# One PSUM tile for a pair of heads' scores, filling passes tied two attention steps up, and a gate phase without GpSimd, in a three-mixer decoder layer on one core

## Chip, core, metric

One core of a Trainium2 chip runs the whole kernel. The metric is the time of one execution on the device, in microseconds (us). The engines are called by name or by the profile's short names: TensorE (PE, with its weight loads as PEld), VectorE (DVE), ScalarE (ACT), GpSimd (POOL), SyncE (SP, which issues the transfers).

## What is computed

One pre-norm layer over 512 tokens of width 1024, float32 throughout. Three attention mixers run side by side on the normalised input, each with eight heads of 64: A (block-sparse; with 512 tokens it is plain causal attention), B (three dilated sliding windows, mixed by their softmax denominators) and C (window 128, two shared key heads, learned sinks). Each mixer's output is multiplied by a SiLU gate, projected to 1024, multiplied by a sigmoid gate, summed with the others and projected once more:

```python
branches = jnp.stack([o_a.reshape(b, s, W_BR) * jax.nn.silu(ga),
                      o_b.reshape(b, s, W_BR) * jax.nn.silu(gb),
                      o_c.reshape(b, s, W_BR) * jax.nn.silu(gc)], axis=2)
br = jnp.einsum('bsiw,iwd->bsid', branches, w_branch[l])
gates = jax.nn.sigmoid(gate_logits.reshape(b, s, N_BRANCH, D_MODEL))
merged = jnp.sum(gates * br, axis=2)
x = x + jnp.einsum('bsd,de->bse', merged, w_out[l])
```

## The kernel before

**Arithmetic.** Every float32 operand of a matmul is split in two fp32r parts: `hi` (a rounding copy, `split_hi`, on ScalarE, line 131) and `lo = x - hi` (`split_lo`, line 136, on VectorE or GpSimd). A product is three passes: hi with hi, hi with lo, lo with hi. All weights go through this split once, in `load_w`, which gives every fourth `lo` (every second for three jobs) to GpSimd.

**Stages.** The start normalises x and transposes it (`start_x`) and makes the bias table (`start_bias`). Then ten attention units run in the order A0 W0 R0 Z0 A1 W1 R1 Z1 C0 C1; each is one half (four heads) of mixer A, of one of B's three windows (W, R, Z), or of C. A unit is projected (`unit_project`, lines 484 to 486 are its passes) and then attended: A and W by `pair_attention`, R and Z by `residue_attention`, C by `shared_attention`. Last comes the gate phase: a list of jobs, each a product of x with 512 columns of gate weights (`gl`, `raw`) or a branch product with `w_branch` (`br`), and the output projection (line 1069).

**An attention step.** In `pair_attention`, `scores(p, t)` takes one 128-row block t of two heads e = 0, 1, which lie on rows 0 to 63 and 64 to 127: three passes for each, written in turns (line 639), into two PSUM tiles of one bank under the tag `sc`, of which there are two buffers. VectorE adds the bias and takes the row minimum (line 568), ScalarE exponentiates (line 569), TensorE transposes the result (line 659), both engines split it, and `weigh_values` multiplies by the values (line 594). A half unit has 8 `scores` steps: p = 0, 1 and t = 0 to 3. Their width is 256 columns in W, and 256, 256, 384, 512 in A. `residue_attention` writes one bank per head for all four t (line 735); `shared_attention` takes a new `sc` tile for every block (lines 701 and 702).

**Order of the work.** Instructions are traced in program order and queued by the builder's scheduler: on each engine, what is ready by its own clock goes first, earlier-traced ones before later ones. The next unit's projection is a generator of three passes at a time ("filling"). For the units in `RATION` some of it is traced ahead, and the rest between the steps, a share after each; `issue_after` allows those passes only behind the step's last TensorE instruction:

```python
for pe in steps:
    got += share
    with tc.issue_after(pe.ins):
        while got >= 1:
            next(fill, None)
            got -= 1
```

C0 and C1 are filled with the first gate columns (`raw_columns`).

**The gate phase.** From the third job on, the products of 512 x 1024 by 1024 x 512 are made from seven smaller ones (Strassen-like, `fast_cols`, line 347): `fast_x` makes combinations of x once, `fast_weights` makes combinations of each job's weights and splits them (lines 291 to 299 and 136). Of a job's seven `lo` parts three are GpSimd's, as is one subtraction (line 296); of `fast_x`, three sums (line 311) and two `lo` parts. `fast_cols` sums the products out of PSUM banks a, b, c, d (lines 364 to 381; c has the tag `sc`). `silu` multiplies sigmoid by the raw gate on GpSimd (line 993) and by the mixer's output on VectorE (line 994). The branch products go to four banks, one of them `sc` (lines 1041 to 1043), and are gated at lines 1049 to 1052.

GpSimd keeps, before and after, the power for the norms (line 142), the sums of B's outputs (line 968) and memsets.

Of the kernel before, what the change touches and what calls it, by code (L numbers as in the profile page):

```python
# [9 lines left out]
F32 = mybir.dt.float32  # L10
# [15 lines left out]
ORAWS = 3  # L26
KEEP = 0
# [72 lines left out]
def body(tc, x, ln_g, w_in, qk_g, sinks, w_branch, w_out, rel_bias, c_ident, c_onehot, c_mask, c_expand, out):  # L100
# [9 lines left out]
    with top:  # L110
# [68 lines left out]
        def start_x():  # L179
# [8 lines left out]
            xts = []  # L188

# [7 lines left out]
            for t in range(NT):  # L197
# [11 lines left out]
                for g in range(2):  # L209
                    gs = slice(g * 512, g * 512 + 512)  # L210
                    V.scalar_tensor_tensor(xn[:, gs], xt[:, gs], r, lng[g], ALU.mult, ALU.mult)
                    pt = ps.tile([128, 4, 128], F32, name="pt", tag=("tr", "sc")[g])
                    for k in range(4):
                        T.transpose(pt[:, k], xn[:, (g * 4 + k) * 128 : (g * 4 + k + 1) * 128], ident)
                    dh = xhi[:, g * 4 : g * 4 + 4, t * 128 : (t + 1) * 128]
                    dl = xlo[:, g * 4 : g * 4 + 4, t * 128 : (t + 1) * 128]
                    split_hi(dh, pt)
                    split_lo(dl, pt, dh)
            return w

        def start_bias():
# [4 lines left out]
            rp = ps.tile([32, 64], F32, name="rp", tag="sc")  # L226
# [4 lines left out]
            for kinds in (("A", "W"), ("C", "R", "Z")):  # L231
# [9 lines left out]
                for k in kinds:  # L241
                    for c in range(0, SPAN[k][0], 512):
                        m = min(512, SPAN[k][0] - c)
                        o = OFF[k] + c - c0
                        pf = ps.tile([8, 512], F32, name="pf", tag="sc")
                        T.matmul(pf[:, :m], rt[:, HEAD0[k] : HEAD0[k] + 8], oh[:, o : o + m], start=True, stop=True)
                        V.tensor_tensor(fb[:, o : o + m], pf[:, :m], mk[:, o : o + m], ALU.add)
# [24 lines left out]
        def fast_weights(src):  # L272
# [17 lines left out]
            parts(L[0, 0], G)  # L290
# [4 lines left out]
            parts(L[0, 1], G)  # L295
            G.tensor_tensor(L[0, 0], L[0, 0], L[1, 0], ALU.subtract)
            parts(L[0, 0], V)
            parts(L[1, 1], G)
# [4 lines left out]
        def fast_x():  # L303
# [18 lines left out]
            full(X, 0, 1, G)  # L322
            full(Y, 0, 0, G)
            full(Z, 1, 1, V)
            V.tensor_tensor(Y, X, Y, ALU.subtract)
            t1 = parts(Y, "t1", G)
# [4 lines left out]
            full(Y, 1, 0, G)  # L331
            V.tensor_tensor(Y, Y, Z, ALU.subtract)
            t4 = parts(Y, "t4", G)
# [4 lines left out]
        def fast_cols(sets, xs, res, put):  # L338
# [13 lines left out]
            def bank(tag):  # L352
                return ps.tile([128, 2, 256], F32, name="fc", tag=tag)
# [31 lines left out]
        raws = {}  # L385
        jobs = [("raw", br, c0) for br, c0 in (("B", GB), ("A", GA))]
# [9 lines left out]
        def job_load(n):  # L396
# [3 lines left out]
            if ty in ("raw", "gl"):  # L400
                c0 = v if ty == "raw" else GL + v * D + u * 512
                if n < PLAIN:
                    return load_w([win_piece(c0, 512)], KT, every=2)
                return fast_weights(lambda i, k: win[:, 4 * k : 4 * k + 4, c0 + 256 * i : c0 + 256 * i + 256])
            if ty == "br":
                return load_w([(512, lambda k0, k1: wbr[v, :, k0:k1, u * 512 : u * 512 + 512])], 4)
            return load_w([(1024, lambda k0, k1: wou[:, k0:k1, :])], KT)
# [20 lines left out]
        with att:  # L428
# [172 lines left out]

            def window(kind, t):
# [3 lines left out]
            def pair_attention(kind, hf, u, stat, oraw):  # L606
# [10 lines left out]
                def scores(p, t):  # L617
# [15 lines left out]
                    scs = [ps.tile([128, 512], F32, name="sc", tag="sc") for _ in range(2)]  # L633
# [49 lines left out]
            def shared_attention(kind, hf, u, stat, oraw):  # L683

                qh, ql, kh, kl, vh, vl = u
                bw = 256
                for j in range(4):
# [5 lines left out]
                    for t in range(NT):  # L693
# [3 lines left out]
                        sc = ps.tile([128, 512], F32, name="sc", tag="sc")  # L697
# [20 lines left out]
            def residue_attention(kind, hf, u, stat, oraw):  # L718
# [3 lines left out]
                for p in range(2):  # L722
                    scs, bts = [], []
                    for e in range(2):
# [3 lines left out]
                        scs.append(ps.tile([128, NT, 128], F32, name="sc", tag="sc"))  # L728
# [143 lines left out]
            for ui, (kind, hf, gi) in enumerate(units):  # L872
# [24 lines left out]
                if name in RATION:  # L897
# [8 lines left out]
                    got = 0.0  # L906
                    for pe in steps:
                        got += share
                        with tc.issue_after(pe.ins):
# [73 lines left out]
        def silu(br):  # L983

            with tc.issue_after(last_exp[0].ins):
                for hf in range(2):
# [3 lines left out]
                    for p in range(2):  # L990
                        sg = qkv.tile([128, S], F32, name="sil", tag="qn", bufs=3)
                        A.activation(sg, raw[:, p], AF.Sigmoid)
                        G.tensor_tensor(sg, sg, raw[:, p], ALU.mult)
# [5 lines left out]

        wnext = jw[2]  # L1000
# [13 lines left out]
        for n in range(2, len(jobs) - 1):  # L1014
# [19 lines left out]
            else:  # L1034
                br = "ABC"[i]
                for dc in range(4):
                    po = ps.tile([128, 512], F32, name="po", tag=("pj", "sc", "tr", "po")[dc])
# [22 lines left out]
        tags_ps = ["pj", "pj", "tr", "tr", "sc", "sc", "po", "po"]  # L1060
        acc = [ps.tile([128, 512], F32, name="acc", tag=tags_ps[i]) for i in range(8)]
# [48 lines left out]
```

## Time and profile before

| what | value |
|---|---|
| median of 3 runs | 831.88 us (831.68 to 831.96) |
| the profiled execution | 831.55 us |
| its span on the core | 829.8 us |
| instructions | 12661 |
| mean granted TensorE clock | 0.982 of full speed |

A page shows one profiled execution. A matmul's end is modelled and runs into the next one's start, so the step from start to start tells what a pass costs, and busy times are the union. "Idle before <-X" is idle time of the engine that X's end stopped. A granted clock of 1.00 is full speed.

### The profile page before, as it was taken

How to read it: one execution, taken by the hardware profiler on the slowest of the kernel's cores; microseconds unless marked ns; L12 is line 12 of the kernel's file. 1: busy time of each engine (PE TensorE's matmuls, PEld its weight loads, DVE VectorE, ACT ScalarE, POOL GpSimd, SP SyncE). 2: the span in 40 equal slices, each digit the busy share in tenths (PEclk: the TensorE clock that was granted, in tenths of full speed). 3: DMA queues.
4: the chain of work that ended last, by engine and by line, in shares of the span. 5: the costliest groups of instructions: out<-in, count | busy, mean ns of one | idle time of the engine just before them, and what ended most of it. 6: DMA issues, size and time to landing. Idle time of an engine off the chain costs nothing.

```text
span 829.8 us, 12661 instructions
## 1 busy us (share of the span) xinstructions
PE 793.0 (96%) x4727; PEld 669.0 (81%) x4727; DVE 517.2 (62%) x1039; ACT 432.4 (52%) x938; POOL 247.8 (30%) x139
## 2 busy tenths in 40 slices
PE   7999999999988999999999799898998999999997
PEld 4887887788878678877887678786898899989886
DVE  6755663555465767336555387779779676978612
ACT  4634663557578365356665956673454244445300
POOL 4413102012311330111132162235547343652100
PEclk9999999999999999999999899999999899999999
DMA  9454144151331243504431221505044234236302
GB/s 260 142 153 104 52 115 140 55 180 40 102 108 49 54 134 66 182 5 145 124 104 49 66 59 50 189 4 177 26 128 127 84 95 128 82 121 196 112 24 101
DMA packets 67329, 85.73 MB, mean 103 GB/s; under 512 B 4899, under 2 KB 53155, under 8 KB 67268
## 3 DMA queue, kind: packets, MB, share of 16 engines
q1 hardware_dynamic: 67268, 84.93, 34.1%
q8 instruction: 37, 0.61, 0.3%
q14 instruction: 24, 0.20, 0.1%
HBM read 75.41 MB, written 9.50 MB: 102 GB/s over the span
## 4 chain that ended last, share of the span: by engine, by line
PE 79%; DVE 9%; ACT 6%; issue 3%; DMA 2%; POOL 1%; SPq 0%; DVEq 0%; ACTq 0%; POOLq 0%
PE fc L347 12%; PE pj L484 11%; PE pj L486 11%; PE pj L485 11%; PE acc L1069 5%; PE sc L639 4%; PE po L594 3%; DVE wlo L136 2%; PE po L1041 2%; PE po L1042 2%; PE po L1043 2%; PE tr L659 2%; PE pj L267 2%; PE pj L269 2%; PE pj L268 2%
## 5 line engine op out<-in xcount | busy, mean ns | idle before, releaser
L484 PE MATMUL pj<-whi,xhi 128*128 128x512 f32 (+1 forms) x576 | 202.1, 351 | 2.2 <-DVE whi L133 1.2
L486 PE MATMUL pj<-whi,xlo 128*128 128x512 f32 (+1 forms) x576 | 197.4, 343 | 0.0
L485 PE MATMUL pj<-wlo,xhi 128*128 128x512 f32 (+1 forms) x576 | 197.2, 342 | 0.0
L136 POOL TENSOR_TENSOR wlo<-w,whi 128x1024 fp32r<-128x1024 f32 x43 | 111.9, 2606 | 192.4 <-ACT whi L131 191.1
L131 ACT CAST whi<-w 128x1024 fp32r<-128x1024 f32 x108 | 112.1, 1049 | 59.8 <-PE fc L347 16.9
L142 POOL TENSOR_TENSOR rr<-rv,mhalf 128x8 f32<-128x8 f32 (+2 forms) x40 | 66.1, 1653 | 211.5 <-DVE rv L140 205.0
L484 PEld LDWEIGHTS pj<-whi,xhi 128*128 128x128 f32 x576 | 109.7, 190 | 17.5 <-ACT xhi L131 1.6
L486 PEld LDWEIGHTS pj<-whi,xlo 128*128 128x128 f32 x576 | 109.5, 190 | 13.9 <-issue 1.7
L485 PEld LDWEIGHTS pj<-wlo,xhi 128*128 128x128 f32 x576 | 109.7, 190 | 12.1 <-issue 0.5
L136 DVE TENSOR_TENSOR wlo<-w,whi 128x1024 fp32r<-128x1024 f32 x67 | 92.2, 1380 | 30.9 <-ACT whi L131 30.5
L136 DVE TENSOR_TENSOR ptlo<-tr,pthi 128x128 fp32r<-128x128 f32 (+3 forms) x112 | 50.7, 457 | 39.7 <-ACT pthi L131 36.5
L131 ACT CAST pthi<-tr 128x128 fp32r<-128x128 f32 (+3 forms) x112 | 44.1, 398 | 37.1 <-PE tr L659 17.5
L347 PE MATMUL fc<-xhi,whi 128*128 128x256 f32 x192 | 55.3, 288 | 4.9 <-DVE fh L368 4.9
L347 PE MATMUL fc<-xhi,wlo 128*128 128x256 f32 x192 | 54.7, 285 | 0.0
L347 PE MATMUL fc<-xlo,whi 128*128 128x256 f32 x192 | 54.7, 285 | 0.0
L500 DVE TENSOR_REDUCE ss<-sq 128x8 f32<-128x512 f32 (+2 forms) x40 | 25.7, 642 | 42.9 <-ACT sq L498 42.7
L347 PEld LDWEIGHTS fc<-xhi,whi 128*128 128x128 f32 x192 | 37.1, 193 | 6.3 <-DVE fh L368 5.5
L511 DVE TENSOR_TENSOR qn<-qn,rr 128x512 f32<-128x512 f32 (+1 forms) x36 | 29.1, 808 | 20.0 <-POOL rr L142 19.6
L496 ACT COPY qn<-pj 128x512 f32<-128x512 f32 (+1 forms) x36 | 20.5, 570 | 39.2 <-PE pj L486 34.9
L267 PE MATMUL pj<-xhi,whi 128*128 128x512 f32 x96 | 40.0, 417 | 0.0
L136 DVE TENSOR_TENSOR wlo<-sm,whi 128x1024 fp32r<-128x1024 f32 x18 | 32.9, 1829 | 11.4 <-ACT whi L131 11.2
L269 PE MATMUL pj<-xhi,wlo 128*128 128x512 f32 x96 | 38.1, 397 | 1.4 <-DVE wlo L136 1.4
(242 smaller groups left out, 1804.7 us busy)
## 6 DMA issues: line engine op xcount, KB each, us to landing
w<-in_w_in SPq DMA_DIRECT2D x54, 512.0 KB, 4.2
w<-in_w_in SPq DMA_DIRECT2D x72, 256.0 KB, 3.7
w<-in_w_branch SPq DMA_DIRECT2D x12, 512.0 KB, 3.3
vscr<-vn SPq DMA_DIRECT2D x16, 256.0 KB, 3.2
w<-in_w_out SPq DMA_DIRECT2D x8, 512.0 KB, 5.1
osp<-oraw SPq DMA_DIRECT2D x6, 512.0 KB, 2.8
oback<-osp SPq DMA_DIRECT2D x6, 512.0 KB, 4.7
xt<-in_x SPq DMA_DIRECT2D x4, 512.0 KB, 6.7
```

Source lines behind the costliest of these rows:

```text
L131: A.copy(dst, src)
L136: eng.tensor_tensor(dst, src, hi.bitcast(F32), ALU.subtract)
L142: G.tensor_tensor(r, v, mhalf[:, :n], ALU.pow)
L267: T.matmul(psum, a, xhi[:, k, :], start=(k == 0), stop=False)
L269: T.matmul(psum, wlo(k)[:, c : c + 128], xhi[:, k, :], start=False, stop=(k == KT - 1))
L347: T.matmul(psum[:, c], w[:, k, cs], x_[:, k, :], start=(first and c == 0 and k == 0 and q == 0), stop=(c == 1 and k == 3 and q == 2), skip ...
L484: T.matmul(pj[:, :ncol], xh, whi(k), start=(k == 0), stop=False)
L485: T.matmul(pj[:, :ncol], xh, wlo(k), start=False, stop=False)
L486: T.matmul(pj[:, :ncol], xl, whi(k), start=False, stop=(k == KT - 1))
L511: V.tensor_tensor(q3[:, :nq], q3[:, :nq], r[:, :nq].unsqueeze(2).broadcast_to([128, nq, 64]), ALU.mult)
L639: pe = T.matmul(scs[e][:, :wm], q[rows, p, qs], k[rows, p, ks], start=(n == 0), stop=(n == 2), skip_group_check=True,)
L1069: T.matmul(acc[t * 2 + e], part[k // 2][:, k % 2, tsl], wo[q](k)[:, es], start=(k == 0 and q == 0 and part is mhi), stop=(k == KT - 1 and ...
```

## The change

The two score banks become one PSUM tile of 128 x 2 x 512 with one buffer, `score_tile`: in `pair_attention` one for each step, in `residue_attention` one for each pair of heads, in `shared_attention` one for the whole half with the two halves used in turn. In the start and in the gate phase one such tile stands for the two `sc` buffers, and the bias table's tiles go to the tag `po`. The filling passes are tied to the step two places up (`LAG`). In the gate phase every GpSimd operation is given to VectorE; of the raw weights' `lo` parts GpSimd gets every fourth and no longer every second, of the branch and output weights' none.

```diff
+LAG = 2
...
+            xsc = ps.tile([128, 2, 512], F32, name="xsc", tag="sc", bufs=1)
...
-                    pt = ps.tile([128, 4, 128], F32, name="pt", tag=("tr", "sc")[g])
+                    if g:
+                        pt = xsc[:, t % 2].rearrange("p (k c) -> p k c", k=4)
+                    else:
+                        pt = ps.tile([128, 4, 128], F32, name="pt", tag="tr")
...
-                        pf = ps.tile([8, 512], F32, name="pf", tag="sc")
+                        pf = ps.tile([8, 512], F32, name="pf", tag="po")
...
-            parts(L[0, 0], G)
+            parts(L[0, 0], V)
...
-            parts(L[0, 1], G)
-            G.tensor_tensor(L[0, 0], L[0, 0], L[1, 0], ALU.subtract)
+            parts(L[0, 1], V)
+            V.tensor_tensor(L[0, 0], L[0, 0], L[1, 0], ALU.subtract)
             parts(L[0, 0], V)
-            parts(L[1, 1], G)
+            parts(L[1, 1], V)
...
-            full(X, 0, 1, G)
-            full(Y, 0, 0, G)
+            full(X, 0, 1, V)
+            full(Y, 0, 0, V)
...
-            t1 = parts(Y, "t1", G)
+            t1 = parts(Y, "t1", V)
...
             def bank(tag):
+                if tag == "sc":
+                    return gsc[0][:, 0].rearrange("p (c n) -> p c n", c=2)
                 return ps.tile([128, 2, 256], F32, name="fc", tag=tag)
...
-                    return load_w([win_piece(c0, 512)], KT, every=2)
+                    return load_w([win_piece(c0, 512)], KT)
...
-                return load_w([(512, lambda k0, k1: wbr[v, :, k0:k1, u * 512 : u * 512 + 512])], 4)
-            return load_w([(1024, lambda k0, k1: wou[:, k0:k1, :])], KT)
+                return load_w([(512, lambda k0, k1: wbr[v, :, k0:k1, u * 512 : u * 512 + 512])], 4, every=1000)
+            return load_w([(1024, lambda k0, k1: wou[:, k0:k1, :])], KT, every=1000)
...
+            def score_tile():
+
+                return ps.tile([128, 2, 512], F32, name="sc", tag="sc", bufs=1)
...
-                    scs = [ps.tile([128, 512], F32, name="sc", tag="sc") for _ in range(2)]
+                    sc = score_tile()
+                    scs = [sc[:, e] for e in range(2)]
...
+                both = score_tile()
                 for j in range(4):
...
-                        sc = ps.tile([128, 512], F32, name="sc", tag="sc")
+                        sc = both[:, t % 2]
...
-                    scs, bts = [], []
+                    bts = []
+                    both = score_tile()
+                    scs = [both[:, e].rearrange("p (t c) -> p t c", t=NT) for e in range(2)]
...
+                    past = []
                     for pe in steps:
                         got += share
-                        with tc.issue_after(pe.ins):
+                        past.append(pe)
+                        with tc.issue_after(past[-1 - LAG if len(past) > LAG else 0].ins):
...
-                        G.tensor_tensor(sg, sg, raw[:, p], ALU.mult)
+                        V.tensor_tensor(sg, sg, raw[:, p], ALU.mult)
...
+        gsc.append(ps.tile([128, 2, 512], F32, name="fsc", tag="sc", bufs=1))
...
-                    po = ps.tile([128, 512], F32, name="po", tag=("pj", "sc", "tr", "po")[dc])
+                    tg = ("pj", "sc", "tr", "po")[dc]
+                    po = gsc[0][:, 1] if tg == "sc" else ps.tile([128, 512], F32, name="po", tag=tg)
...
+        asc = ps.tile([128, 2, 512], F32, name="acc", tag="sc", bufs=1)
+        acc[4:4] = [asc[:, 0], asc[:, 1]]
```

## Rows read from the trace of the kernel before

**Rows 1.** The page, part 1: busy time of each engine, its share of the span, its instructions.

```profile
PE 793.0 (96%) x4727; PEld 669.0 (81%) x4727; DVE 517.2 (62%) x1039; ACT 432.4 (52%) x938; POOL 247.8 (30%) x139
```

**Rows 2.** The table by stretch: from:to in us, length, then the busy time (and the number of instructions) of PE, PEld, DVE, ACT and POOL, the mean granted TensorE clock, the share of the DMA engines and GB/s.

```profile
78.00:138.00 60.00, 59.92 (x389) 50.43 (x389) 35.16 (x93) 32.42 (x84) 10.04 (x6) 1.00 0.42 118
138.00:181.00 43.00, 41.00 (x251) 33.59 (x250) 22.37 (x58) 24.71 (x64) 7.35 (x4) 0.96 0.29 90
266.00:338.00 72.00, 71.11 (x434) 56.41 (x434) 49.39 (x126) 37.88 (x97) 18.65 (x13) 1.00 0.35 96
338.00:396.00 58.00, 55.02 (x326) 44.96 (x327) 25.79 (x64) 29.14 (x70) 11.34 (x6) 1.00 0.35 105
444.00:475.00 31.00, 26.07 (x163) 21.02 (x160) 15.88 (x61) 25.95 (x64) 7.37 (x4) 0.89 0.26 77
475.00:535.00 60.00, 56.78 (x345) 47.71 (x344) 46.15 (x143) 37.76 (x110) 22.86 (x14) 0.97 0.28 80
552.00:781.00 229.00, 221.18 (x1439) 200.33 (x1438) 184.60 (x169) 104.45 (x130) 109.76 (x45) 0.99 0.37 113
```

**Rows 3.** The list of waits of TensorE over the whole span: waiting line <- releaser: us in total, times, the longest.

```profile
PE fc L347 <- DVE fh L368: 4.9, 3, 3.2
...
PE sc L701 <- DVE sl L568: 2.1, 1, 2.1
PE sc L639 <- DVE sm L568: 2.0, 2, 1.0
PE tr L659 <- ACT qf L547: 1.9, 3, 0.8
```

**Rows 4.** TensorE in order of time, in unit A0: start, us, engine, line, operation, shape, how many; of a pair of heads, and of one head alone.

```profile
84.75 0.39 PE L639 MATMUL sc<-khi,qhi 64*128 64x256 f32 x2
...
85.09 0.28 PE L639 MATMUL sc<-khi,qlo 64*128 64x256 f32 x2
...
87.35 0.38 PE L639 MATMUL sc<-khi,qhi 64*128 64x256 f32 x1
...
87.69 0.28 PE L639 MATMUL sc<-khi,qlo 64*128 64x256 f32 x1
```

**Rows 5.** Line 639 alone (score passes of pair_attention), in the stretches of the units A0, W0, A1, W1: from:to, length, busy time (passes), granted clock, DMA share, GB/s. The pair at the end of the first stretch is the first of W0 and is in the second row too.

```profile
78.00:115.00 37.00, 11.37 (x54) 1.00 0.38 96
114.00:169.00 55.00, 7.42 (x48) 0.97 0.32 96
266.00:310.00 44.00, 8.49 (x48) 1.00 0.33 96
330.00:383.00 53.00, 7.73 (x48) 1.00 0.34 106
```

**Rows 6.** TensorE in order of time, in unit A1: first and last passes of a pair of 384 columns and of one of 512.

```profile
276.79 0.45 PE L639 MATMUL sc<-khi,qhi 64*128 64x384 f32 x2
...
277.25 0.34 PE L639 MATMUL sc<-khi,qlo 64*128 64x384 f32 x2
...
282.85 0.51 PE L639 MATMUL sc<-khi,qhi 64*128 64x512 f32 x2
...
283.42 0.40 PE L639 MATMUL sc<-khi,qlo 64*128 64x512 f32 x2
```

**Rows 7.** Line 568 alone (the softmax's first half on VectorE) in the same four stretches, their sum.

```profile
sum 189.00, DVE 26.90; mean DVE 6.72
```

**Rows 8.** TensorE in order of time, in unit Z1: the score passes of the second pair, the first group of them and the last.

```profile
450.08 0.71 PE L735 MATMUL sc<-kf,qf 64*128 64x128 f32 x4
...
452.77 0.71 PE L735 MATMUL sc<-kf,qf 64*128 64x128 f32 x6
```

**Rows 9.** Groups of instructions of GpSimd from 552 to 781 us: line, engine, operation, out<-in, shape, xcount | busy us, mean ns | idle before, releasers.

```profile
L136 POOL TENSOR_TENSOR wlo<-w,whi 128x1024 fp32r<-128x1024 f32 x23 | 63.9, 2786 | 71.1 <-ACT whi L131 71.1
L993 POOL TENSOR_TENSOR sil<-sil,graw 128x512 f32<-128x512 f32 x12 | 22.4, 1888 | 6.4 <-ACT sil L992 6.4
L296 POOL TENSOR_TENSOR w<-w,w 128x1024 f32<-128x1024 f32 x6 | 15.1, 2518 | 23.0 <-DVE sm L293 12.2 <-issue 7.8 <-PE fc L347 3.0
```

**Rows 10.** VectorE in order of time, from 633 us on.

```profile
633.34 0.67 DVE L994 TENSOR_TENSOR oback<-sil,oback 128x512 f32<-128x512 f32 x1
633.94 1.21 DVE L136 TENSOR_TENSOR wlo<-w,whi 128x1024 fp32r<-128x1024 f32 x1
...
637.03 3.21 DVE L136 TENSOR_TENSOR wlo<-sm,whi 128x1024 fp32r<-128x1024 f32 x1
640.16 3.39 DVE L136 TENSOR_TENSOR wlo<-w,whi 128x1024 fp32r<-128x1024 f32 x1
```

**Rows 11.** Groups of instructions of VectorE from 552 to 781 us, columns as in rows 9.

```profile
L136 DVE TENSOR_TENSOR wlo<-sm,whi 128x1024 fp32r<-128x1024 f32 x18 | 32.9, 1829 | 11.4 <-ACT whi L131 11.2
L136 DVE TENSOR_TENSOR wlo<-w,whi 128x1024 fp32r<-128x1024 f32 x20 | 29.1, 1461 | 4.4 <-ACT whi L131 4.4
L1052 DVE TENSOR_TENSOR mg<-mg,gsg 128x512 f32<-128x512 f32 x15 | 17.3, 1169 | 0.1
L994 DVE TENSOR_TENSOR oback<-sil,oback 128x512 f32<-128x512 f32 x12 | 14.1, 1200 | 0.0
L299 DVE TENSOR_TENSOR sm<-w,sm 128x1024 f32<-128x1024 f32 x6 | 14.1, 2346 | 0.1
```

**Rows 12.** TensorE from 640 to 650 us: length, busy time, granted clock, DMA share, GB/s.

```profile
640.00:650.00 10.00, 6.77 (x36) 0.67 0.56 172
```

More of the change, by code (lines that the diff above doesn't have):

```diff
@@ L225, in start_bias @@
             nc.sync.dma_start(rb[:40, :], rel_bias)
-            rp = ps.tile([32, 64], F32, name="rp", tag="sc")
+            rp = ps.tile([32, 64], F32, name="rp", tag="po")
             T.transpose(rp, rb, ident[:64, :64])
@@ L330, in fast_x @@
             t2 = parts(Z, "t2", V)
-            full(Y, 1, 0, G)
+            full(Y, 1, 0, V)
             V.tensor_tensor(Y, Y, Z, ALU.subtract)
-            t4 = parts(Y, "t4", G)
+            t4 = parts(Y, "t4", V)
             split_hi(t3[0], X)
@@ L385, in body @@
         raws = {}
+        gsc = []
         jobs = [("raw", br, c0) for br, c0 in (("B", GB), ("A", GA))]
@@ L727, in residue_attention @@
                         bts.append(bt[:, :128])
-                        scs.append(ps.tile([128, NT, 128], F32, name="sc", tag="sc"))
                     for t in range(NT):
@@ L1057, in body @@
                         split_lo(mlo[q][:, dc % 2], mg[q][:, dc % 2], mhi[q][:, dc % 2])
-        tags_ps = ["pj", "pj", "tr", "tr", "sc", "sc", "po", "po"]
-        acc = [ps.tile([128, 512], F32, name="acc", tag=tags_ps[i]) for i in range(8)]
+        tags_ps = ["pj", "pj", "tr", "tr", "po", "po"]
+        acc = [ps.tile([128, 512], F32, name="acc", tag=t) for t in tags_ps]
+        asc = ps.tile([128, 2, 512], F32, name="acc", tag="sc", bufs=1)
+        acc[4:4] = [asc[:, 0], asc[:, 1]]
         wo = wnext
```

## The prediction

> **What bounds the kernel now.** I read the busy shares first [rows 1]: TensorE is busy 793.0 of 829.8 us, VectorE 62%, ScalarE 52%, GpSimd 30%. So a saving counts where it takes work off TensorE, or some of the 36.8 us in which it idles. The table by stretch [rows 2] says where these lie: in the stretches of the four pair-attention units (78 to 181 and 266 to 396 us) TensorE idles 5.9 of 233 us, in a dilated unit without filling (444 to 475) 4.9 of 31, around the C heads (475 to 535) 3.2, in the gate phase (552 to 781) 7.8. The list of TensorE's waits [rows 3] names the releasers of the longest. There the change must earn its time, or in the width of the work itself: TensorE's timeline [rows 4] shows the score matmuls of two heads, each on 64 rows, as "x2" in the time that one head's take alone: six passes of 256 columns from 84.75 to 85.09 + 0.28 = 85.37, 0.62 us; three alone from 87.35 to 87.69 + 0.28, also 0.62. A pass without its partner wastes half the array.
>
> **Score banks as one tile.** In pair_attention the two heads' banks now come free together. The builder's scheduler places an instruction when its operands and buffers are ready; before, one bank came free a softmax ahead of the other, and its three passes went off alone. Now it finds all six ready at once. What is there to save: the passes' busy time by unit is 11.37, 7.42, 8.49 and 7.73 us [rows 5]; the first holds one pair of the next unit (54 passes for 48), 0.62 us, so 10.75. All paired, a W unit has 8 steps of 0.62 = 4.96, an A unit 4 of 0.62, 2 of 0.80 (276.79 to 277.59) and 2 of 0.97 (282.85 to 283.82) [rows 6] = 6.02. Saved: A0 4.7, W0 2.5, A1 2.5, W1 2.8, together 12.5 us. Bounds: 0 where the freed time becomes waiting, 12.5 where filling takes it up. In the stretches that begin A0 and A1, TensorE is busy 59.92 of 60 and 71.11 of 72 us [rows 2], so I take their 7.2 whole; those of W0 and W1 have idle time (2.0 and 3.0), so I take half of 5.3, 2.6. Term: **-9.8**.
>
> The wait that this adds: a pair waits for the second softmax too, and what the compiled order has behind it on TensorE (transposes, filling) waits with it. The units' 64 softmaxes take 26.9 us [rows 7], 0.42 each; over all 32 pair steps 13.4 us at most. It costs nothing while filling passes stand between two steps, as now.
>
> In residue_attention the second pair's scores now wait for the first pair's last softmax, where they began in pieces, x4 at 450.08 and the last x6 at 452.77 [rows 8]. A later start costs nothing under filling (R0, R1), and up to 452.77 - 450.08 = 2.7 us in each of Z0 and Z1, which have none; nothing there either if ScalarE, busy 25.95 of 31 us, ends last. Bounds 0 to 5.4; nearer ScalarE's row: **+0.7**. In the C heads the two halves of one tile alternate as two buffers did: 0, covered by the filling between steps; were the halves tied together, 32 steps would wait a softmax each. The tiles of the x, bias and output stages keep their number of banks: 0. In the gate phase bank c is now always the same one; only where two product jobs adjoin (raw C, then a gate) can that be felt, and there the next job's first product runs before c is written: 0, or one eviction if VectorE is late.
>
> **Filling tied two steps up.** Filling passes that stood behind attention step n may now stand behind n-2, so ahead of a step that waits. No instruction is added. What they can fill is idle time in front of steps: sc 2.1 and 2.0, tr 1.9, sum 6.0 us [rows 3]. The number of filling passes is the same, so what is used early is missing later. Bounds: +2, if the sc waits of W0 and W1 are met a second time behind it, to -6.0; **-2**, nearer nothing, because all four units together idle only 5.9 us.
>
> **Gate phase without GpSimd.** From 552 to 781 us GpSimd runs 23 weight splits, 12 SiLU products and 6 subtractions [rows 9], and five sums and splits of `fast_x` at most (the diff). On VectorE a 1024-wide operation takes 1.21 us and a 512-wide 0.67 where GpSimd rests [rows 10], so they add 34 x 1.21 + 12 x 0.67 = 49.2 us to its queue. Against that stands what GpSimd costs VectorE now: beside GpSimd's splits the same VectorE split took 3.21 and 3.39 us [rows 10]. Mean against clean in the five largest groups [rows 11]: wlo from sm 18 x 0.62 = 11.1, wlo from w 20 x 0.25 = 5.0, L299 6 x 1.14 = 6.8, L1052 15 x 0.50 = 7.5, L994 12 x 0.53 = 6.4, sum 36.8. So VectorE goes from 184.6 us [rows 2] to 197.0 of 229 at most, and a split that took 2.8 us on GpSimd takes 1.2. What changes is lateness: TensorE's waits on L368 (4.9 us, the longest 3.2 [rows 3]) come when evictions stand behind a pile of splits, as the two above, and the granted clock of 640 to 650 us, behind that longest wait, is 0.67 [rows 12]: 3.3 us lost. So 7.8 + 3.3 = 11.1 us can go. But VectorE's queue now carries GpSimd's splits too, and L368 to L381, for which TensorE waits, stand behind them; and SiLU's products, the input of the branch matmuls. At the pile: 2 slow splits took 6.6 us; these and the three that GpSimd ran beside them take 5 x 1.21 = 6.1 in a row, hardly less. I take **-4**, bounds -11.1 and +5 (rival b).
>
> The Trainium skill, "SBUF — State Buffer", section "Who interferes with whom", says that a VectorE instruction with two SBUF inputs and a GpSimd instruction that reads SBUF exclude each other, the second blocked until the first ends. By that rule the 36.8 us come back whole and the term stays; if the slow operations are slow for a reason of their own, it is rival b. The rows agree with the rule as far as they go (3.21 and 3.39 against 1.21).
>
> Of the raw weights' splits three move to VectorE in C0 and C1: 3.6 us beside its 46.15 of 60 there [rows 2], covered by filling, 3.6 if not. No DMA is added or moved; weight loads start when their buffers are split, on VectorE's time now.
>
> **Sum.** -9.8 + 0.7 - 2 - 4 = -15.1. The profiled execution took 831.55 us (829.8 of span and 1.75 around it), 0.33 under the median of the runs. A measurement of this kernel tells 0.2%, 1.7 us, so I leave that out: 831.55 - 15.1 = **816.5 us**.
>
> **Rivals.** (a) Slower: the softmax becomes the path. Where no filling is left each pair step waits 0.42 us more, and idle time lowers the clock: in 138 to 181 us 2.0 idle go with 0.96 granted over 43 us, 0.86 lost for each idle one; in 338 to 396 3.0 idle with none [rows 2]. All 32 steps at 0.86: -12.5 - 4 + 13.4 x 1.86 = +8.4, 840 us; with no loss of clock 828. It decides from 22 of 32 steps on (16.5 of 24.9). For it: TensorE's waits on softmax in W0 and W1, 2.0 us [rows 3]. Against it: the full stretches of A0 and A1, and filling that may go ahead. Where it decides, 837.
> The Trainium skill, "TensorEngine Tiling (Array Packing)", section "Performance Considerations", says that packing speeds up TensorE but not the reading of PSUM, which may become the bottleneck. The trace bears that out for two waits of 1.0 us.
>
> (b) VectorE becomes the bound of the gate phase, because GpSimd is not what slows it. Then 184.6 + 49.2 = 233.8 us stand in 229: +5 at least instead of -4, some +10 with evictions late, 825.5 to 830.5 us. Against it: 1.21 wherever GpSimd rests.
>
> (c) The pairing does not come about, because filling passes that are ready slip between the six: -9.8 falls away, 826 us. For it: TensorE's queue is ordered by readiness, and even now most passes are not written apart, only placed apart.
>
> **Chances.** Forecast 0.55 (its own range 807 to 824), (c) 0.10, (b) 0.14, (a) 0.17, orders that fit none 0.04. Faster by over 0.2%: 0.55 + 0.09 + 0.08 = 0.72; within 0.2%: 0.08, the edges of (a), (b) and (c); slower: 0.20, from (a) with 0.14 and the late ends of the others. All gains whole give 831.55 - 12.5 - 6.0 - 11.1 = 802, which takes three best ends at once; below 806 I leave some 0.05. The upper end, 834, takes in (b), (c) and the edge of (a), and leaves out some 0.13.
>
> **What would show it.** Right: L639 as x2 throughout, its busy time by unit near 6.0 and 5.0 us; VectorE's splits at 1.2 us from 552 us on and its busy time there near 197 or below; no 3 us wait on L368 and no slice at 0.67 granted clock; waits on softmax no longer than now. Wrong: L639 still in threes; TensorE's waits on L568 over 10 us in all; VectorE above 90% from 552 to 781 us with L368 to L381 named as releasers.

## The result, and the profile after

The changed kernel takes 807.6 us (median; 804.37 to 810.36) against 831.78 us before: 24.2 us less, ratio 0.9717 [0.9672, 0.9762]. The prediction was 816.5 us, in a range of 806 to 834. The direction held, and so did the mechanisms of the gains; two of their terms were too small. One term was wrong: the tile costs time in the C heads and the gate phase, which the prediction put at nothing, and the other two parts have to cover most of it. The profiled execution took 808.76 us, span 807.0. Line numbers have moved: score passes L639 are L652, the softmax L568 is L576, `fast_x` L347 is L352, evictions L368 to L381 are L375 to L388, splits L136 are L137. The page's busy shares [rows 1]:

```profile
PE 783.0 (97%) x4727; PEld 663.4 (82%) x4727; DVE 515.6 (64%) x1088; ACT 432.4 (54%) x938; POOL 128.2 (16%) x90
```

Where the time went is seen best if both spans are cut at the same events: C0's first score pass, C0's normalising transposes (L781 before) and the first `acc` matmul. The first three stretches of before (columns as in [rows 2]):

```profile
0.00:472.22 472.22, 450.81 (x2638) 367.92 (x2638) 261.43 (x678) 273.92 (x662) 109.61 (x79) 0.98 0.37 106
472.22:523.57 51.35, 48.14 (x301) 41.01 (x302) 41.08 (x132) 32.42 (x92) 21.63 (x14) 0.97 0.23 60
523.57:780.93 257.36, 249.52 (x1599) 224.27 (x1598) 201.66 (x217) 122.16 (x182) 114.12 (x46) 0.99 0.36 114
```

And of after:

```profile
0.00:462.82 462.82, 444.49 (x2637) 365.45 (x2638) 264.94 (x680) 273.54 (x662) 110.03 (x78) 0.98 0.36 109
462.82:514.53 51.71, 50.33 (x307) 41.56 (x305) 39.77 (x130) 33.20 (x91) 15.72 (x12) 1.00 0.20 56
514.53:758.11 243.58, 243.58 (x1596) 220.53 (x1594) 198.74 (x265) 121.78 (x181) 2.40 (x1) 1.00 0.38 121
```

The attention up to C0 is 9.4 us shorter, C0's heads are level (+0.4), C1 with the gate phase is 13.8 us shorter, and what is left at the end is 48.9 us long in both. In the third stretch TensorE is busy in every one of 243.58 us at full clock. Of the 13.8 us, 7.8 were idle time (257.36 - 249.52); the other 5.9 are busy time. Up to 3.4 of them were lost to the clock, whose lower level is 1.2 of 2.4 GHz: cut in slices of 10 us, the stretch of before is under full clock in two only, 0.67 from 640 to 650 us [rows 12] and 0.99 from 650 to 660, both behind the longest stall. Some 2 more are no gain but a shift: nine passes of the first gate columns (0.23 us each from start to start) stand in C0 now. C0 of before and of after, passes into the tile `pj` alone:

```profile
472.20:523.60 51.40, 32.89 (x159) 0.97 0.23 60
```

```profile
462.80:514.50 51.70, 33.78 (x168) 1.00 0.20 56
```

So C0, level in length, does some 2 us more work. The slice that ran at 0.67 runs at full clock now:

```profile
640.00:650.00 10.00, 10.00 (x70) 9.15 (x69) 8.03 (x11) 4.43 (x5) 0.00 (x0) 1.00 0.31 95
```

The score passes alone (line 652) in the units W0, A1 and W1, in answer to [rows 5]:

```profile
115.00:167.00 52.00, 6.36 (x48) 3.93 (x48) 1.00 0.42 123
260.00:305.00 45.00, 6.77 (x48) 3.94 (x48) 1.00 0.32 96
325.00:379.00 54.00, 6.89 (x48) 4.06 (x48) 1.00 0.35 111
```

They were 7.42, 8.49 and 7.73 us. The units A and W have 96 pairs of such passes, three in each of 32 steps (below they are also called rows). In TensorE's order of time 85 of the 96 now stand side by side (as "x2"), against 44 before.

VectorE's groups in the gate phase, columns as in [rows 9], in answer to [rows 11]:

```profile
L137 DVE TENSOR_TENSOR wlo<-w,whi 128x1024 fp32r<-128x1024 f32 x43 | 52.0, 1220 | 13.2 <-ACT whi L132 13.2
L137 DVE TENSOR_TENSOR wlo<-sm,whi 128x1024 fp32r<-128x1024 f32 x18 | 21.9, 1219 | 1.7 <-ACT whi L132 1.7
L1071 DVE TENSOR_TENSOR mg<-mg,gsg 128x512 f32<-128x512 f32 x15 | 10.1, 683 | 0.0
...
L304 DVE TENSOR_TENSOR sm<-w,sm 128x1024 f32<-128x1024 f32 x6 | 7.3, 1218 | 0.0
```

Each takes the price that was clean before: 1219 ns for 1829, 683 for 1169, 1218 for 2346. VectorE does GpSimd's work as well and is busy 2.9 us less.

### The profile page after: what moved, and what is told of

It is laid out like the page before. It is cut to its first block, busy times and chain, and to the rows that moved or that the text cites. A ratio compares the mean times of both kernels' runs of the same rounds, so it can differ in the third digit from the quotient of the medians.

```text
span 807.0 us, 12636 instructions
## 1 busy us (share of the span) xinstructions
PE 783.0 (97%) x4727; PEld 663.4 (82%) x4727; DVE 515.6 (64%) x1088; ACT 432.4 (54%) x938; POOL 128.2 (16%) x90
## 4 chain that ended last, share of the span: by engine, by line
PE 88%; DVE 4%; ACT 4%; issue 2%; DMA 1%; POOL 0%; SPq 0%; DVEq 0%; ACTq 0%; POOLq 0%
PE pj L492 13%; PE pj L493 12%; PE pj L494 12%; PE fc L352 10%; PE acc L1090 5%; PE fsc L352 4%; PE po L602 3%; PE sc L652 3%; PE pj L272 2%; PE pj L274 2%; PE pj L273 2%; PE po L1060 2%; PE po L1061 2%; PE po L1062 2%; PE tr L672 2%; PE tr L549 2%
## 5 line engine op out<-in xcount | busy, mean ns | idle before, releaser
L493 PE MATMUL pj<-wlo,xhi 128*128 128x512 f32 (+1 forms) x576 | 199.2, 346 | 0.0
L137 DVE TENSOR_TENSOR wlo<-w,whi 128x1024 fp32r<-128x1024 f32 x93 | 117.6, 1273 | 39.1 <-ACT whi L132 38.4
L493 PEld LDWEIGHTS pj<-wlo,xhi 128*128 128x128 f32 x576 | 111.1, 193 | 12.4 <-issue 0.8
L494 PEld LDWEIGHTS pj<-whi,xlo 128*128 128x128 f32 x576 | 111.0, 193 | 12.4 <-issue 0.5
L137 DVE TENSOR_TENSOR ptlo<-tr,pthi 128x128 fp32r<-128x128 f32 (+3 forms) x112 | 50.9, 458 | 30.6 <-ACT pthi L132 22.4
L137 POOL TENSOR_TENSOR wlo<-w,whi 128x1024 fp32r<-128x1024 f32 x17 | 41.1, 2419 | 98.5 <-ACT whi L132 98.5
L576 DVE CUSTOM_DVE_ANT_0 lg<-sc,bt 128x128 f32<-128x128 f32 (+2 forms) x96 | 28.5, 335 | 24.6 <-PE sc L652 12.2
L577 ACT ACTIVATE lg<-lg,sm 128x128 f32<-128x128 f32 (+1 forms) x80 | 32.8, 411 | 14.0 <-DVE sm L576 13.7
L352 PE MATMUL fc<-xlo,whi 128*128 128x256 f32 x144 | 40.2, 279 | 0.0
L352 PE MATMUL fc<-xhi,wlo 128*128 128x256 f32 x144 | 40.2, 279 | 0.0
L352 PE MATMUL fc<-xhi,whi 128*128 128x256 f32 x144 | 40.2, 279 | 0.0
L273 PE MATMUL pj<-xlo,whi 128*128 128x512 f32 x96 | 37.9, 395 | 0.0
```

What stands on the lines that cost most here:

```text
L137: eng.tensor_tensor(dst, src, hi.bitcast(F32), ALU.subtract)
L273: T.matmul(psum, a, xlo[:, k, :], start=False, stop=False)
L352: T.matmul(psum[:, c], w[:, k, cs], x_[:, k, :], start=(first and c == 0 and k == 0 and q == 0), stop=(c == 1 and k == 3 and q == 2), skip ...
L493: T.matmul(pj[:, :ncol], xh, wlo(k), start=False, stop=False)
L494: T.matmul(pj[:, :ncol], xl, whi(k), start=False, stop=(k == KT - 1))
L577: last_exp[0] = A.activation(lg, lg, AF.Exp, bias=mcol, scale=-1.0, accum_out=lcol)
```

## The experiments

The change has three parts, here called tile (one score tile for a pair), lag (filling two steps up) and gate (no GpSimd work). Six kernels besides before tell them apart; the ratios are to runs of before on the same chip. "To C0" is the span's start to C0's first score pass in the profiled run, "from C0" the rest of its span.

| kernel | parts | median us | ratio to before | to C0 | from C0 |
|---|---|---|---|---|---|
| before | none | 831.78 | 1 | 472.2 | 357.6 |
| e1_gate | gate | 819.68 | 0.9858 [0.9832, 0.9884] | 472.4 | 345.3 |
| e3_lag | lag | 825.89 | 0.9939 [0.9908, 0.9969] | 467.1 | 355.7 |
| e2_tile | tile | 837.55 | 1.0077 [1.0050, 1.0104] | 463.4 | 371.3 |
| e8_gatelag | gate, lag | 811.72 | 0.9773 [0.9753, 0.9793] | 468.2 | 341.8 |
| e4_nolag | tile, gate | 821.57 | 0.9877 [0.9853, 0.9901] | 464.9 | 354.6 |
| after | all | 807.6 | 0.9717 [0.9672, 0.9762] | 462.8 | 344.1 |

**One part alone, and one part undone.** e1_gate is the kernel before with the change's hunks in `fast_weights`, `fast_x`, `load_w`'s callers and the SiLU product, and nothing else:

```diff
-            parts(L[0, 0], G)
+            parts(L[0, 0], V)
...
-                        G.tensor_tensor(sg, sg, raw[:, p], ALU.mult)
+                        V.tensor_tensor(sg, sg, raw[:, p], ALU.mult)
```

> The kernel before with the gate phase's GpSimd operations on VectorE and nothing else. Theory (the gate phase gained by itself, because GpSimd's reads no longer slow VectorE): the stretch from the end of C0 to the output projection shrinks by 11 to 14 us, time 818 to 821 us, TensorE idle in it under 1 us. Rival (the gate phase gained because the attention ahead of it ends in a better order, or because the fixed score bank reorders its products): 826 to 831 us.

It took 819.68 us; the theory held. The whole gain lies from C0 on (357.6 to 345.3): C0 is 1.4 us shorter (51.35 to 49.96), and the stretch from C0's transposes to the first `acc` matmul 10.9 (257.36 to 246.44).

e2_tile has the score tile of the change, with the filling tied to the step just issued and GpSimd at work in the gate phase:

```diff
+                sc = score_tile()
+                scs = [sc[:, e] for e in range(2)]
...
+LAG = 0
```

> The kernel before with the score banks as one tile (and the tiles of the other stages that follow from it), filling still tied to its own step, gate phase with GpSimd. Theory (pairing saves TensorE's work and nothing takes it back): 20 of 96 pairs of passes stand together in the compiled order before, 88 now; time 822 to 825 us, line of the scores down by 8 to 12 us of busy time. Rival (the pair waits for the second softmax and the filling behind it waits too): TensorE's waits on the softmax grow by 5 us or more, 828 to 832 us.

It is slower than before, 837.55 us, and the theory fell. Up to C0 the tile gives 8.8 us (472.2 to 463.4), as it should; 2.6 of them are in Z1, which has no filling. From C0 on it loses 13.7. The two stretches of the loss, C0's heads (51.35 us before), and C1 with the gate phase (257.36):

```profile
463.35:519.82 56.47, 50.04 (x302) 41.45 (x302) 43.17 (x136) 33.85 (x96) 21.89 (x14) 0.97 0.21 61
519.82:785.85 266.03, 254.91 (x1600) 228.35 (x1598) 204.31 (x214) 122.50 (x177) 109.91 (x46) 0.96 0.33 108
```

TensorE's longest waits in them (waiting line <- releaser: us in total, times, longest):

```profile
PE po L602 <- DVE ptlo L137: 6.4, 2, 3.7
PE fsc L352 <- DVE gsg L1070: 3.1, 1, 3.1
...
PE fsc L352 <- DVE mg L1068: 1.7, 1, 1.7
...
PE fsc L352 <- DVE graw L381: 1.1, 1, 1.1
```

The waits for the softmax (line 576) are 2.3 us over the whole span, 4.1 before, so the rival's reason does not hold either. The first line is the attention steps' wait for the split of their transposed scores. In C0 that split stood behind two VectorE operations that ran beside GpSimd's (a sum and a weight split, from 510.11 to 515.76 us):

```profile
510.41 3.15 DVE L137 TENSOR_TENSOR wlo<-w,whi 128x1024 fp32r<-128x1024 f32 x1
513.49 2.30 DVE L942 TENSOR_TENSOR ex<-sl,nsk 128x16 f32<-128x16 f32 x1
```

In e4_nolag, where GpSimd has no work there, the same two take 1.22 and 0.17 us. `fsc` is the tile that stands for the two `sc` buffers in the gate phase, one half for bank c and one for a branch product. L352, which writes bank c, waits for VectorE 5.9 us in three waits, and 4.8 of them (L1070, L1068) end when VectorE has read the other half. In e4_nolag L352 waits for nothing.

e3_lag ties the filling two steps up in the kernel before:

```diff
-                        with tc.issue_after(pe.ins):
+                        past.append(pe)
+                        with tc.issue_after(past[-1 - LAG if len(past) > LAG else 0].ins):
```

> The kernel before with the filling tied two steps up and nothing else. Theory (it only moves filling into the short waits in front of steps): -1 to -3 us, 829 to 831 us. Rival (it carries a good part of the gain of the whole change): 824 to 827 us.

825.89 us, 5 to 6 us better: near the bound of -6.0 and not the -2 that was taken. Its runs spread from 821.54 to 831.39 us, and the interval of the ratio stands for a gain of 2.6 to 7.7 us.

e4_nolag is the changed kernel with `LAG = 0`.

> The changed kernel with the filling tied to its own step again. Theory (the three parts add up): 808 to 811 us. Rival (filling two steps up is what covers the pair's longer wait for both softmaxes): 813 us or more, with TensorE waiting for the softmax in W0 and W1.

821.57 us. Without the lag 14 of the 24 us are gone, and the tile adds nothing to the gate part alone (819.68). What fails is seen in C0:

```profile
464.94:525.27 60.33, 56.36 (x318) 45.93 (x318) 42.48 (x140) 35.83 (x99) 16.23 (x12) 0.92 0.21 57
```

Against 51.71 us in the changed kernel: 4.0 us idle instead of 1.4, and a clock of 0.92, so that 318 passes take 56.4 us where 307 take 50.3. (The eleven more passes, about 1.5 us, are then missing behind C0.) TensorE's order of time in that stretch, from one filling pass (`pj`) to the next:

```profile
513.41 0.39 PE L274 MATMUL pj<-xhi,wlo 128*128 128x512 f32 x1
...
515.21 0.44 PE L723 MATMUL tr<-idr,lg 128*128 128x128 f32 x2 [0.83 <-ACT lg L577]
516.38 0.38 PE L602 MATMUL po<-ptlo,vhi 128*128 128x256 f32 x1 [0.73 <-DVE ptlo L137]
...
518.12 0.58 PE L602 MATMUL po<-ptlo,vhi 128*128 128x256 f32 x1 [0.41 <-DVE ptlo L137]
...
519.33 0.63 PE L272 MATMUL pj<-xhi,whi 128*128 128x512 f32 x1
```

For 5.9 us no filling stands in the queue. Short attention steps wait one after another, and behind these waits passes of 512 columns last 0.63 us for 0.39: the granted clock has fallen. In e2_tile the longest such stretch is 8.2 us. Length alone does not make the loss: TensorE is idle for 2.0 of the 5.9 us here and for 4.5 of the 8.2, but only for 0.1 in a stretch of 4.1 us without filling in the changed kernel (503.69 to 507.84) and for 1.1 in one of 6.2 us before (487.95 to 494.12), where other work stands ready.

What keeps the steps from running ahead of each other is the tile itself. Its halves are used in turn, but no step's scores begin before the softmax of the step ahead has read the other half. VectorE's softmax (L576) and TensorE's next scores (L715) in e4_nolag, then the same in the kernel before (lines 568 and 701), where two steps' scores stand finished while VectorE is late:

```profile
516.24 0.34 DVE L576 CUSTOM_DVE_ANT_0 lg<-sc,bt,nsk 128x128 f32<-128x128 f32 x1
516.72 0.32 PE L715 MATMUL sc<-khi,qhi 128*128 128x256 f32 x1
```

```profile
517.64 0.28 PE L701 MATMUL sc<-khi,qhi 128*128 128x256 f32 x1
519.05 0.37 PE L701 MATMUL sc<-khi,qhi 128*128 128x256 f32 x1
521.72 0.30 DVE L568 CUSTOM_DVE_ANT_0 lg<-sc,bt,nsk 128x128 f32<-128x128 f32 x1
```

Of the 32 steps of C0 and C1, 15 to 17 begin with a softmax still outstanding in the four kernels without the tile, and none in the ten with it. So when VectorE is late, the steps of C run one by one.

With the lag, filling may stand inside such a stretch. The end of C0 in the changed kernel:

```profile
511.75 0.40 PE L272 MATMUL pj<-xhi,whi 128*128 128x512 f32 x1
511.98 0.28 PE L602 MATMUL po<-pthi,vhi 128*128 128x256 f32 x1
512.10 0.40 PE L273 MATMUL pj<-xlo,whi 128*128 128x512 f32 x1
```

**Gate and lag without the tile.** e8_gatelag is e1_gate with the diff of e3_lag.

> The kernel before with the filling passes tied two steps up and the gate phase without GpSimd, but the score banks as before: what the tile for the pair is worth once both others are there. If the parts add up (filling alone 6 us, gate alone 12 us): 812 to 815 us, and the tile is worth 5 to 7 us on top. Rival (the filling two steps up pays only where the pair holds both banks at once, 14 us with it): it gives little here, 816 to 820 us, and tile and filling are worth 9 to 12 us together and nothing apart. Third: 806 to 809 us, the tile is worth nothing.

811.72 us: the two parts add up within the intervals (0.9858 x 0.9939 gives 0.9798, measured 0.9773), and the tile is worth some 4 to 5 us on top, a little less than the 5 to 7 expected. The table shows it as a balance: 5.4 us won up to C0, 2.3 lost from C0 on, even with both other parts there. (From C0 on, profiled runs of the changed TensorE program agree well: 344.1, 343.9 in e6_writes, 344.0 in e7_whole.)

**Why the gate part gains.** Two kernels put work back on GpSimd without changing TensorE's program. e5_reads adds, for each weight set in the gate phase, a subtract of two inputs whose result nobody reads:

```diff
+                dum = gp.tile([128, 4, 256], F32, name="dum", tag="dum", bufs=1)
+                G.tensor_tensor(dum, hi.bitcast(F32), hi.bitcast(F32), ALU.subtract)
```

> The changed kernel with 42 more GpSimd instructions in the gate phase: after each weight set's high parts are made, GpSimd subtracts them from themselves over 1024 columns into a scratch tile, and nobody reads the result. TensorE's program is unchanged. Theory (GpSimd's two-operand arithmetic slows the VectorE instructions beside it, and that is most of what the gate part gained): VectorE's 1024-column splits of the gate phase go from a mean of 1.22 us back to 1.6 us or more, TensorE waits there again, and the time is 814 to 820 us. Rival (the gate part gained because the chain of sums and splits no longer passes from VectorE to GpSimd and back): the splits may be slower, but TensorE goes on without a wait and the time stays within 3 us of the changed kernel, 805 to 811 us.

e6_writes puts a copy of 8 columns and two memsets in the same places:

```diff
+                G.tensor_copy(dum[:, 0, 0:8], hi[:, 0, 0:8].bitcast(F32))
+                G.memset(dum, 0.0)
+                G.memset(dum, 0.0)
```

> As the kernel with the 42 subtracts, but in each place GpSimd copies 8 columns and sets the scratch tile to zero twice, so that it is as busy but reads next to nothing. If what slows VectorE is GpSimd's reading, VectorE's splits stay at 1.2 to 1.3 us and the time at 806 to 810 us. If any work of GpSimd slows VectorE, the splits are at 1.6 us or more and the time is with that of the subtracts, 814 to 820 us. If neither matters for the time, both are within 3 us of the changed kernel.

e5_reads took 851.4 us, ratio 1.0259 [1.0235, 1.0283]; e6_writes 806.42 us, 0.9707 [0.9687, 0.9728]. The theory on reading held in direction, and was far too small in size. From C0's transposes to the first `acc` matmul, e5_reads:

```profile
510.64:800.18 289.54, 260.17 (x1595) 233.22 (x1594) 258.58 (x265) 120.94 (x181) 110.56 (x43) 0.95 0.31 101
```

and e6_writes:

```profile
512.40:755.98 243.58, 243.58 (x1596) 220.53 (x1594) 198.78 (x265) 121.82 (x181) 114.33 (x127) 1.00 0.37 121
```

GpSimd is as busy in the one as in the other (110.56 and 114.33 us). VectorE's work takes 59.8 us longer beside the reads and not 0.1 longer beside the writes. VectorE in order of time in e5_reads, where GpSimd has four of its subtracts in a row, from 616.69 to 630.32 us:

```profile
617.65 1.21 DVE L137 TENSOR_TENSOR wlo<-sm,whi 128x1024 fp32r<-128x1024 f32 x1
...
622.82 2.91 DVE L306 TENSOR_TENSOR sm<-w,sm 128x1024 f32<-128x1024 f32 x1
625.66 2.91 DVE L137 TENSOR_TENSOR wlo<-w,whi 128x1024 fp32r<-128x1024 f32 x1
```

VectorE first goes on at its clean price, and then L306 and L137 take 1.7 us more each. TensorE waits for it again, its list of waits there:

```profile
PE fc L354 <- DVE wlo L137: 11.1, 5, 4.0
PE fsc L1062 <- DVE gsg L390: 5.9, 3, 3.4
```

so 29.4 us idle, and 16.6 us more busy time at a clock of 0.95. (In the kernel before GpSimd was at work for as long, 114.12 us, but on work that VectorE was spared; in e5_reads it comes on top, so the loss here is not what GpSimd cost before.) The rule of the Trainium skill cited in the prediction ("SBUF — State Buffer", "Who interferes with whom") says further that a VectorE instruction with two SBUF inputs contends with GpSimd instructions that read SBUF and not with those that only write it. These two runs agree with both halves.

**All 96 rows side by side.** e7_whole raises the priority of the six passes:

```diff
+                    with tc.high_priority():
                         for n, (q, k) in enumerate(((qh, kh), (qh, kl), (ql, kh))):
```

> The changed kernel with the six score passes of a pair raised in priority, so that in all 96 rows of the A and W units the two heads' passes stand side by side in TensorE's order (87 of 96 in the changed kernel, 20 of 96 before). Theory (what the tile gives is that passes run two at a time): the nine rows that are left gain some 0.1 to 0.4 us each, 804 to 807 us. Rival (raising the scores moves them ahead of filling that they then wait beside): 808 to 814 us.

805.86 us, ratio 0.9706 [0.9685, 0.9728]. Beside e6_writes (806.42 us, TensorE's program as in the changed kernel) that is no difference. (In the order of time 85 of 96 pairs stand side by side in the changed kernel and 44 before, not the 87 and 20 of the expectation; here it is all 96.) Line 652 (653 here) from 40 to 480 us, the kernel before, the changed one, and e7_whole:

```profile
sum 440.00, PE 34.98 PEld 21.68; mean PE 34.98 PEld 21.68
```

```profile
sum 440.00, PE 26.54 PEld 15.64; mean PE 26.54 PEld 15.64
```

```profile
sum 440.00, PE 22.55 PEld 14.03; mean PE 22.55 PEld 14.03
```

The last eleven pairs take another 4.0 us of work from TensorE, and the time does not show it. TensorE's busy time up to C0 is only 0.9 us below that of e6_writes (440.05 and 440.95), for the profiled run of e7_whole lost more to the clock in the units without filling: the slices of 10 us under full clock before C0 (230 to 260 and 440 to 460 us) add up to 8.5 us by their granted clocks, in e6_writes to 5.1. Whether the pairing brought that about, or the spread that two runs of one program show (below), stays open.

**Where the lag works.** It reaches only the units that have a ration of filling: A0, W0, W1 and C. (The expectation of e10_lagpair names A1 and the residue units too; they have none.)

```diff
+                    lag = LAG if kind == "C" else 0
```

> The changed kernel with the filling two steps up in the C unit alone; in the pair units it is tied to the step just issued, as before. Theory (what the lag gives back is the loss in C's head loop: the segment from C0's first score to the gate's transposes is 60.3 us without lag and 51.7 with it, while all that stands ahead of C0 differs by 2 us): nearly all of the 14 us stays, 807 to 812 us, and C0 is at 51 to 53 us. Rival (the lag works in the pair units, where the score tile's only buffer is handed on from row to row): 815 to 821 us.

```diff
+                    lag = LAG if kind != "C" else 0
```

> The mirror image: two steps up in the pair units (A0, W0, A1, W1 and those of the residue groups) and none in C. Theory: the loss in C stays, 815 to 820 us, with C0 at 58 to 61 us. Rival: 807 to 812 us, with C0 near 52 us.

813.01 us [0.9764, 0.9790] with the lag in C alone, 815.98 us [0.9803, 0.9831] with it in the pair units alone. The first lies 1 us above what the theory gave (807 to 812), the second in its range (815 to 820), but its reason was half the truth: the lag works in both places, 8.6 us in C and 5.6 in the pair units, and the two sum to the 14. C0 takes 51.75 us with the lag in C and 60.50 without; from C0 on it is 344.2 and 354.7. Up to C0 e10_lagpair takes 460.0 us and e9_lagc 467.7.

With `LAG = 1` and `LAG = 4`:

> The changed kernel with the filling one step up in place of two. If one step of slack is what a stalled step needs (the waits that the lag covers were 1 to 3.7 us, and a step of C is about 2 us): 808 to 814 us, between none (821.6) and two. If the place of the filling alone matters and not the slack: within 3 us of two steps up, 805 to 811 us.

> The changed kernel with the filling four steps up. If two steps already cover what is late (TensorE waits 0 in the gate phase and some 14 us in all the attention units): within 3 us of the changed kernel, 805 to 811 us. If more slack covers more: 801 to 805 us. If filling that runs ahead leaves the ends of the units bare (residue units' start and end already went up by 1 to 4 us with two steps): 810 to 815 us.

One step gives 821.53 us, as much as none; four give 806.1, as much as two. One step is not half of two: C0 has the full gain already (51.72 us), and A0 with W0 lose it, 144.4 us for 132.9 without lag and 127.5 with two. TensorE there, at one step:

```profile
44.83:189.27 144.44, 131.46 (x812) 108.56 (x811) 74.08 (x186) 69.56 (x172) 25.59 (x15) 0.96 0.36 107
```

13.0 us idle, for 2.8 with two steps, and a clock of 0.96. The longest waits are those of attention steps, 4.3 us in four for the softmax (L576) and 2.6 for a split ahead of the values (L602). One of the others, in order of time:

```profile
95.77 0.49 PE L672 MATMUL tr<-idr,late 128*128 128x128 f32 x3
98.17 0.39 PE L492 MATMUL pj<-whi,xhi 128*128 128x256 f32 x1 [1.91 <-DVE vlo L137]
```

Here it is the filling that waits: the pass next in the queue needs the bank `pj`, which VectorE's split of the values (`vlo`) still reads. So the number of steps is no dial over these four settings; each value makes the builder's scheduler lay out another order. Four steps also end up elsewhere (C0 57.70 us, C1 with the gate phase 239.6 instead of 243.6) with nearly the same sum.

## Why the prediction was right, and where it was not

**Pairing (-9.8).** Right in mechanism, nearly right in size, and incomplete: not all pairs came about, and W0 and W1 have 6.4 and 6.9 us where all pairs side by side were to give 5.0. The passes' busy time fell by 8.4 us (34.98 to 26.54) and the attention up to C0 by 9.4, by 8.8 with the tile alone. With all pairs side by side (e7_whole) it falls by 12.4, the 12.5 of the prediction's working. TensorE's wait on the softmax at the score passes, 2.0 us [rows 3], is one of 0.2 now; rival (c) is out.

**C heads and bank c (0 and 0).** This step failed. With the tile alone these places cost 13.7 us, more than the pairing gives, and the kernel is slower than before. The prediction took the halves to "alternate as two buffers did" and named as the other case "were the halves tied together, 32 steps would wait a softmax each". They are tied: none of the 32 steps begins before the softmax of the step ahead has read its half, where about half of them did before. In the gate phase too, 4.8 of the 5.9 us for which L352 waits end with a read of the other half. TensorE's list of waits hides it in C (0.2 us at L715 in C0), because the whole chain of scores, softmax, transposes and values is late and the wait falls to its other links. Nor was it "covered by the filling between steps": e4_nolag shows 5.9 us in which no filling stands between them. In e2_tile operations made slow beside GpSimd come on top (3.15 us and 2.30 us above). What the tie costs by itself is not shown, for no run gives C two tiles beside the pair's one; nor is it shown why the scheduler puts no filling into the end of C0, where e1_gate (C0 at 50.0 us) goes without for 2.3 us at most.

**Filling two steps up (-2).** Mis-sized: -5 to -6 alone, -8.0 with the gate part there (819.68 to 811.72), -14 with tile and gate. The price was taken from the waits of the kernel before (6.0 us, [rows 3]). It could not hold the waits that the tile itself would create, and it left out what an idle stretch costs behind it, at the lower clock level: in C0 4.0 us idle go with 60.33 us instead of 51.7, a clock of 0.92 and eleven more passes.

**Residue (+0.7).** The later start costs nothing: with the tile alone the four units R0, Z0, R1, Z1 take 156.7 us, 157.8 before. In the changed kernel they take 166.0, for another reason, that filling left over by A0, W0 and W1 runs there now. Line 492 alone has x94 and x70 passes in the two stretches R0 with Z0 and R1 with Z1, x89 and x65 before; with its two sister lines that is some 30 passes more, at 0.23 us from start to start some 7 us. What the lag takes out of the pair units is partly a shift, as "what is used early is missing later" said.

**Gate phase (-4).** Mechanism right, mis-sized: -12.1 us alone (831.78 to 819.68), of which 10.9 in the gate phase and 1.4 in C0 by the traces. That is the bound of -11.1, and its two terms were rightly read: the idle time all but goes (7.8 to 0.9), and the clock's part, read from one slice as 3.3 us, is 3.4 at most over the stretch. The 13.8 of the whole change hold the nine passes that C0 took over. What was short is what GpSimd costs VectorE: it was summed over five groups, 36.8 us; VectorE took on some 49 us of work and ended 2.9 lower, so it was about 52. The remark that a pile without GpSimd takes "hardly less" time is what pulled the term to -4: no pile of that kind is left, and TensorE has not one wait in the phase. Rival (b) is out; e5_reads is what it looks like when GpSimd reads.

**Sum.** -15.1 forecast, -22.8 in the profiled executions (831.55 to 808.76). That the sum is not further off is in part luck: gains of the filling and the gate phase that were taken too small stand against the cost of the tile that was left out. The tile alone came to 837.55 us where rival (a) had 837: the right time for the wrong reason, since the pair units, where it was to happen, were faster (A1 with W1 127.9 us, 131.5 before).

## What to carry to other kernels

Two buffers made into the halves of one tile are no longer two buffers: look whether a step still begins while the other half is being read, and do not go by the list of waits alone. A part that shortens TensorE's work can leave holes elsewhere in a queue that a scheduler lays out; look for stretches without filling, and count the passes behind each hole at the lower clock. Parts measured alone do not add up when one covers the wait that another makes: tile 5.8 us slower alone, 4 to 5 faster on top of the other two. And an engine that looks spare is not free: in e5_reads, where it took nothing off VectorE, 110 us of GpSimd's two-input work cost VectorE 60 us and the kernel 45, and as much time of memsets cost nothing.

## What the runs showed that was not expected

GpSimd loses in the contention too, however little it reads. In e6_writes its copy of 8 columns takes 0.19 us beside a VectorE operation that reads a PSUM bank (L379, `fc`). It takes 3.97 us, from 606.64 to 610.61, while VectorE runs four operations with both inputs in SBUF back to back, and it ends when the next one reads PSUM (L392, `fsc`). The memsets keep their 0.96:

```profile
606.64 3.97 POOL L292 COPY dum<-whi 128x8 f32<-128x8 f32 x1 [2.68 <-ACT whi L132]
...
620.84 0.19 POOL L292 COPY dum<-whi 128x8 f32<-128x8 f32 x1
```

```profile
606.47 1.22 DVE L305 TENSOR_TENSOR w<-w,w 128x1024 f32<-128x1024 f32 x1
...
610.48 0.69 DVE L392 TENSOR_TENSOR gsg<-fsc,fh 128x512 f32<-128x512 f32 x1
...
620.35 0.69 DVE L379 TENSOR_TENSOR fh<-fc,fh 128x512 f32<-128x512 f32 x1
```

Runs of one TensorE program differ by 2 us in one place. Unit Z1, which has no filling, took 28.67 us at a granted clock of 0.76 in the changed kernel and 26.71 us at 0.94 in e6_writes, whose TensorE order is the same:

```profile
434.15:462.82 28.67, 25.43 (x145) 21.28 (x145) 14.02 (x50) 23.32 (x61) 2.89 (x2) 0.76 0.25 78
```

```profile
434.17:460.88 26.71, 22.12 (x145) 17.82 (x144) 13.12 (x47) 22.86 (x61) 2.37 (x1) 0.94 0.26 84
```

So nothing is concluded above from a difference of 2 or 3 us "to C0" between two profiled runs (e4_nolag and e9_lagc, the same program up to there, have 464.9 and 467.7), and the changed kernel's own runs spread from 804.37 us at 0.996 to 810.36 at 0.985.
